# Two-layer hybrid encoder trunk: the split weight buffers begin at eight different 16-byte phases modulo 128 instead of one

## Chip, cores and metric

The kernel runs on one core of one Trainium2 chip. The metric is device time in microseconds of one execution, the median over the runs shown. Ahead of the launch the host only lays the inputs out in memory.

## The reference, cut to what matters

The input x is 512 tokens by 1024 channels in float32. Two layers follow each other, each a mixer and a gated MLP, all with residual adds, and a last RMSNorm. The outer structure, in which `even_mixer` and `odd_mixer` are attention layers with one combined input projection and one output projection each:

```python
h = x + even_mixer(rms_norm(x), w_in, w_out)     # layer 0: sparse top-k attention + chunked attention
h = h + conv_gated_ffn(rms_norm(h), w_up, conv_w, conv_b, w_down)
h = h + odd_mixer(rms_norm(h), w_in, w_out)      # layer 1: forgetting attention + windowed attention
h = h + conv_gated_ffn(rms_norm(h), ...)
y = rms_norm(h)

def conv_gated_ffn(x, w_up, conv_w, conv_b, w_down):
    h = x @ w_up                                  # 1024 -> 2 * 2816
    h = depthwise_causal_conv3(h, conv_w) + conv_b
    g, u = split(h, 2)
    return (silu(g) * u) @ w_down                 # 2816 -> 1024
```

What counts here is the dense products with weights: the input projections of the mixers, their output projections, and the up- and down-projections of the MLPs.

## The kernel before

Tokens lie along the free axis and channels on the partitions. Each product of two float32 matrices is made from three matmuls: both operands are split into a high part, rounded to the type that TensorE streams in one pass (float32r), and a low part, the remainder; `mm3` (L174 to L177) issues high x high at L175, then at L176 and L177 the two mixed products, into one PSUM bank.

**The weights.** `Stream` (from L114) walks a fixed plan of 196 weight tiles, each 128 partitions by up to 1024 words. `issue` loads one tile from HBM into `raw` (L132, two buffers, issued on SyncE), ScalarE copies it, rounded, into `whi` (L135), and VectorE subtracts that from `raw` into `wlo` (L137; for the keys `A1` and `kB`, eight tiles, GpSimd does it). There are four buffers for `whi` and four for `wlo`, used in turn. `ahead` keeps two tiles ready, `get` hands one out as a view of the columns in use. 188 tiles are 1024 words wide; four have 648 (two halves of 324, the indexer's projection, `"i"`) and four have 528 (two halves of 264, the narrow projection of layer 1, `"d"`).

**Who reads them.** In `tok_group` and `tok_wide` the activations `xT` are the stationary operand of the matmul and the weights stream by as the moving one, in rows of 512, 324 or 264 words. In `chan_mm`, `out_half` and the down-projection the weights are the stationary operand, in blocks of 128 x 128, and the activations (`xT`, `yT`, `VS`, `act`) stream by with 512 columns (256 in a few places). Each matmul instruction brings its own load of the stationary operand.

**The order of the work.** Every engine gets its instructions in the order in which the program writes them. In the mixers, dense matmuls are woven between the attention steps as fill (`weave`, `Fill`); in an MLP (`ffn`, from L702) one weight tile serves one block of 128 channels and 24 matmuls; `W.ahead(2)` stands ahead of each. The convolution of the MLP reads and writes with offsets of one and two words: `dst[:, 1:]` at L714 and `dst[:, 2:]` at L716.

**The memory.** Pools lie one behind the other in each partition. The pool of the weights holds `raw`, `whi` and `wlo`, every buffer 4096 bytes, and each of the eight split buffers begins at a multiple of 128 bytes.

Of the kernel before, what the change touches and what calls it, by code (L numbers as in the profile page):

```python
# [11 lines left out]
F32R = mybir.dt.float32r  # L12
# [73 lines left out]
def trunk(ctx, tc, a, out):  # L86
# [5 lines left out]
    wp = ctx.enter_context(tc.tile_pool(name="wts", bufs=4))  # L92
# [24 lines left out]
    class Stream:  # L117
# [4 lines left out]
        def issue(self):  # L122
            key = PLAN[self.pos]
            self.pos += 1
            if key[0] == "i":
                src, w = a["w_i"][key[1]], 2 * NI
            elif key[0] == "d":
                src, w = a["w_d"][key[1]], 2 * ND
            else:
                src, w = a["w"][WIDE_AT[key]], 1024  # L130
            raw = wp.tile([128, 1024], F32, name="raw", tag="raw", bufs=2)
            nc.sync.dma_start(raw[:, :w], src)  # L132
            hi = wp.tile([128, 1024], F32R, name="whi", tag="whi")
            lo = wp.tile([128, 1024], F32R, name="wlo", tag="wlo")
            nc.scalar.activation(hi[:, :w], raw[:, :w], AF.Copy)  # L135
            eng = nc.gpsimd if key[0] in ('A1', 'kB') else nc.vector
            eng.tensor_tensor(lo[:, :w], raw[:, :w], hi[:, :w].bitcast(F32), OP.subtract)  # L137
            self.ready[key] = (hi, lo)
# [1014 lines left out]
```

## Time and profile before

| what | us |
|---|---|
| runs shown | 1284.32 and 1286.52 |
| their median | 1285.42 |
| the profiled execution, its own time | 1287.78 |
| its span, first to last instruction | 1286.1 |

The mean granted clock of TensorE over that span is 0.986 of 2.4 GHz. All instruction times of the trace are from this one execution. PE is TensorE's matmuls, PEld its loads of the stationary operand, DVE is VectorE, ACT is ScalarE, POOL is GpSimd. Names are given as out<-in, and of a matmul's two inputs the moving one comes first. A matmul's record is longer than the spacing of the starts, because matmuls are pipelined; the spacing of the starts is the pace.

### The profile page before, as it was taken

The numbers are of one execution on the slowest core, as the hardware profiler recorded it, in microseconds if no ns is written. First come the engines' busy times: TensorE is split into PE (matmuls) and PEld (weight loads), VectorE is DVE, ScalarE is ACT, GpSimd is POOL, SyncE is SP. The second block draws the span as 40 slices with busy tenths as digits, with TensorE's granted clock in tenths as the row PEclk, the third lists the DMA queues.
The fourth block names the chain that finished last, engine by engine and source line by source line (L and its number), as shares of the span: only waits on it lengthen the run. The fifth ranks groups of instructions, "written<-read, shape, count | busy, mean of one in ns | idle before, by whom it ended". The sixth has DMA issues, their size and how long they took to land. (4 is left out here: it accounts for less than half of the span.)

```text
span 1286.1 us, 15902 instructions
## 1 busy us (share of the span) xinstructions
PE 1265.4 (98%) x5904; PEld 1024.6 (80%) x5904; DVE 826.1 (64%) x1524; ACT 594.0 (46%) x1008; POOL 198.5 (15%) x275
## 2 busy tenths in 40 slices
PE   8999999999999999999999999999999999999997
PEld 7767777777888888888888777778788888888886
DVE  7989865777777777743325566767777777772222
ACT  6545454555544444432224666666644444442221
POOL 3346331212000000000011334311200000000000
PEclk9989999999999999999999999889999999999999
DMA  6322122313223333332222311201333333322321
GB/s 208 85 79 83 34 66 66 99 34 98 86 98 98 99 98 99 96 91 96 96 67 81 115 49 34 66 17 51 100 98 99 99 98 99 96 93 92 98 81 66
DMA packets 34221, 109.61 MB, mean 85 GB/s; under 512 B 4064, under 2 KB 6496, under 8 KB 34144
## 3 DMA queue, kind: packets, MB, share of 16 engines
q1 hardware_dynamic: 34144, 108.60, 27.0%
q8 instruction: 46, 0.75, 0.2%
q14 instruction: 31, 0.25, 0.1%
HBM read 106.49 MB, written 2.10 MB: 84 GB/s over the span
## 5 line engine op out<-in xcount | busy, mean ns | idle before, releaser
L137 DVE TENSOR_TENSOR wlo<-raw,whi 128x1024 fp32r<-128x1024 f32 (+2 forms) x188 | 232.6, 1237 | 152.5 <-ACT whi L135 149.3
L135 ACT ACTIVATE whi<-raw 128x1024 fp32r<-128x1024 f32 (+2 forms) x196 | 204.8, 1045 | 224.3 <-PE acc L176 152.1
L175 PE MATMUL acc<-xT,whi 128*128 128x512 f32 x480 | 191.3, 399 | 0.4 <-ACT xT L229 0.4
L176 PE MATMUL acc<-xT,whi 128*128 128x512 f32 x480 | 188.3, 392 | 1.8 <-DVE xT L230 1.8
L177 PE MATMUL acc<-xT,wlo 128*128 128x512 f32 x480 | 188.0, 392 | 0.0
L212 POOL TENSOR_TENSOR scr<-scr,os 128x512 f32<-128x512 f32 x24 | 34.3, 1430 | 723.2 <-ACT os L210 723.2
L175 PE MATMUL acc<-act,whi 128*128 128x512 f32 (+1 forms) x374 | 140.9, 377 | 0.0
L177 PE MATMUL acc<-act,wlo 128*128 128x512 f32 (+1 forms) x374 | 140.9, 377 | 0.0
L176 PE MATMUL acc<-act,whi 128*128 128x512 f32 (+1 forms) x374 | 140.9, 377 | 0.0
L175 PE MATMUL s<-xT,whi 128*128 128x512 f32 x352 | 137.9, 392 | 0.0
L177 PE MATMUL s<-xT,wlo 128*128 128x512 f32 x352 | 137.0, 389 | 0.0
L176 PE MATMUL s<-xT,whi 128*128 128x512 f32 x352 | 137.0, 389 | 0.0
L175 PEld LDWEIGHTS acc<-xT,whi 128*128 128x128 f32 x480 | 90.8, 189 | 23.5 <-issue 4.8
L176 PEld LDWEIGHTS acc<-xT,whi 128*128 128x128 f32 x480 | 90.8, 189 | 19.9 <-DVE xT L230 2.5
L177 PEld LDWEIGHTS acc<-xT,wlo 128*128 128x128 f32 x480 | 90.6, 189 | 19.4
L175 PE MATMUL acc<-whi,xT 128*128 128x512 f32 (+2 forms) x208 | 84.5, 408 | 0.9 <-ACT whi L135 0.9
L177 PE MATMUL acc<-whi,xT 128*128 128x512 f32 (+2 forms) x208 | 80.7, 389 | 1.3 <-DVE xT L230 1.3
L712 DVE TENSOR_TENSOR ov<-s,R 128x512 f32<-128x512 f32 x44 | 30.4, 692 | 79.9 <-PE s L177 79.9
L182 ACT ACTIVATE act<-scr 128x512 fp32r<-128x512 f32 x44 | 27.8, 631 | 115.7 <-DVE scr L736 115.7
L176 PE MATMUL acc<-wlo,xT 128*128 128x512 f32 (+2 forms) x208 | 80.4, 387 | 0.6 <-DVE wlo L137 0.4
L176 PEld LDWEIGHTS acc<-act,whi 128*128 128x128 f32 x374 | 70.4, 188 | 13.0
L177 PEld LDWEIGHTS acc<-act,wlo 128*128 128x128 f32 x374 | 70.4, 188 | 13.0
(230 smaller groups left out, 2362.1 us busy)
## 6 DMA issues: line engine op xcount, KB each, us to landing
raw<-in_w SPq DMA_DIRECT2D x188, 512.0 KB, 3.5
h<-in_x SPq DMA_DIRECT2D x8, 256.0 KB, 4.1
T<-in_relb SPq DMA_DIRECT2D x8, 256.0 KB, 2.7
raw<-in_w_i SPq DMA_DIRECT2D x4, 324.0 KB, 3.4
raw<-in_w_d SPq DMA_DIRECT2D x4, 264.0 KB, 2.7
out_y<-h SPq DMA_DIRECT2D x4, 256.0 KB, 2.2
out_y<-h SPq DMA_DIRECT2D x2, 384.0 KB, 2.4
ropeC<-in_ropeC SPq DMA_DIRECT2D x2, 256.0 KB, 4.3
```

Of the source, the lines that this page charges most:

```text
L135: nc.scalar.activation(hi[:, :w], raw[:, :w], AF.Copy)
L137: eng.tensor_tensor(lo[:, :w], raw[:, :w], hi[:, :w].bitcast(F32), OP.subtract)
L175: nc.tensor.matmul(o, lh, rh, start=start, stop=False)
L176: nc.tensor.matmul(o, lh, rl, start=False, stop=False)
L177: nc.tensor.matmul(o, ll, rh, start=False, stop=stop)
L182: nc.scalar.activation(dh, src, AF.Copy)
L212: eng.tensor_tensor(ss, ss, sq, OP.add)
L712: nc.vector.tensor_tensor(v, o, R, OP.mult)
```

## The change

The two allocations of a split weight tile become 1040 words wide instead of 1024, and the tile in use is a view of 1024 words that begins 0, 4, 8 or 12 words (0, 16, 32 or 48 bytes) into the buffer. The offset goes to the next value after every fourth tile of the plan. All reads and writes of `whi` and `wlo` go through the view. The instructions, their order, their shapes and their waits are those of before.

```diff
             raw = wp.tile([128, 1024], F32, name="raw", tag="raw", bufs=2)
             nc.sync.dma_start(raw[:, :w], src)
-            hi = wp.tile([128, 1024], F32R, name="whi", tag="whi")
-            lo = wp.tile([128, 1024], F32R, name="wlo", tag="wlo")
+            o = 4 * (self.pos // 4 % 4)
+            hi = wp.tile([128, 1040], F32R, name="whi", tag="whi")[:, o:o + 1024]
+            lo = wp.tile([128, 1040], F32R, name="wlo", tag="wlo")[:, o:o + 1024]
             nc.scalar.activation(hi[:, :w], raw[:, :w], AF.Copy)
             eng = nc.gpsimd if key[0] in ('A1', 'kB') else nc.vector
             eng.tensor_tensor(lo[:, :w], raw[:, :w], hi[:, :w].bitcast(F32), OP.subtract)
```

## Rows read from the trace of the kernel before

**Rows 1.** The page: busy us of each engine, share of the span, instructions.

```profile
PE 1265.4 (98%) x5904; PEld 1024.6 (80%) x5904; DVE 826.1 (64%) x1524; ACT 594.0 (46%) x1008; POOL 198.5 (15%) x275
```

**Rows 2.** Windows in the first MLP's and second MLP's up-projection.

```profile
core 0: us, PE busy (x) PEld busy (x) DVE busy (x) ACT busy (x) POOL busy (x), PEclk, DMA share, GB/s
400.00:500.00 100.00, 100.00 (x443) 82.81 (x442) 73.15 (x92) 46.01 (x56) 0.00 (x0) 1.00 0.31 95
1000.00:1100.00 100.00, 100.00 (x443) 82.84 (x442) 72.62 (x92) 45.67 (x56) 0.00 (x0) 1.00 0.31 97
```

**Rows 3.** Timeline in the first down-projection, TensorE: start us, us, instruction.

```profile
600.05 0.39 PE L175 MATMUL acc<-act,whi 128*128 128x512 f32 x1
...
605.50 0.39 PE L175 MATMUL acc<-act,whi 128*128 128x512 f32 x1
```

**Rows 4.** Timeline in the last column block, with 256 columns, TensorE.

```profile
1273.72 0.28 PE L175 MATMUL acc<-act,whi 128*128 128x256 f32 x1
...
1275.16 0.28 PE L175 MATMUL acc<-act,whi 128*128 128x256 f32 x1
```

**Rows 5.** Instructions on the tile whi: count, ns minimum/median/maximum, first and last start.

```profile
L175 PEld LDWEIGHTS acc<-act,whi x374: 187/188/192, 552.2 to 1276.1; 128*128 128x128 f32 x187
L175 PEld LDWEIGHTS acc<-whi,xT x208: 186/188/192, 6.3 to 818.7; 128*128 128x128 f32 x104
```

**Rows 6.** Waits of TensorE: us in total, times, longest us.

```profile
PE s L175 <- ACT qk L493: 2.0, 1, 2.0
PE acc L176 <- DVE xT L230: 1.8, 2, 1.0
PE s L176 <- POOL qk L494: 1.6, 2, 1.0
...
PE acc L175 <- ACT whi L135: 0.9, 1, 0.9
...
PE acc L176 <- DVE wlo L137: 0.4, 1, 0.4
```

**Rows 7.** Timeline of both narrow projections, TensorE: halves begin at the acc rows.

```profile
20.05 0.31 PE L175 MATMUL acc<-whi,xT 128*128 128x324 f32 x1
...
21.70 0.31 PE L177 MATMUL s<-whi,xT 128*128 128x324 f32 x1
21.84 0.31 PE L175 MATMUL acc<-whi,xT 128*128 128x324 f32 x1
...
23.47 0.31 PE L177 MATMUL s<-whi,xT 128*128 128x324 f32 x1
...
675.04 0.28 PE L175 MATMUL acc<-whi,xT 128*128 128x264 f32 x1
...
676.48 0.28 PE L175 MATMUL acc<-whi,xT 128*128 128x264 f32 x1
...
677.93 0.28 PE L175 MATMUL acc<-whi,xT 128*128 128x264 f32 x1
```

**Rows 8.** Timeline of a stretch of 128-column matmuls, TensorE.

```profile
821.04 0.27 PE L176 MATMUL s<-kdT,qk 64*128 64x128 f32 x1
...
821.82 0.27 PE L177 MATMUL s<-kdT,qk 64*128 64x128 f32 x1
```

**Rows 9.** Groups by line and form: count, busy us, mean ns, idle before and releaser.

```profile
L137 DVE TENSOR_TENSOR wlo<-raw,whi 128x1024 fp32r<-128x1024 f32 x180 | 224.8, 1249 | 139.4 <-ACT whi L135 136.2
L716 DVE SCALAR_TENSOR_TENSOR scr<-ov,cw,scr 128x510 f32<-128x510 f32 x88 | 66.0, 750 | 3.0
L714 DVE SCALAR_TENSOR_TENSOR scr<-ov,cw,scr 128x511 f32<-128x511 f32 x88 | 65.6, 745 | 0.0
...
L187 DVE SCALAR_TENSOR_TENSOR VS<-acc,rs,VS 128x512 fp32r<-128x512 f32 x12 | 8.9, 747 | 10.2 <-ACT VS L186 10.2
...
L135 ACT ACTIVATE whi<-raw 128x1024 fp32r<-128x1024 f32 x188 | 199.3, 1060 | 207.7 <-PE acc L176 136.2 <-PE s L176 40.7 <-DMA raw<-in_w 9.4
```

**Rows 10.** Windows around the two falls of the granted clock; columns as in rows 2.

```profile
73.40:83.60 10.20, 9.18 (x23) 6.64 (x24) 6.47 (x23) 3.00 (x7) 2.66 (x4) 0.51 0.16 50
...
824.00:827.70 3.70, 3.32 (x19) 2.30 (x18) 3.27 (x12) 3.20 (x15) 0.94 (x2) 1.00 0.36 121
827.70:848.20 20.50, 20.50 (x55) 13.98 (x55) 9.62 (x39) 8.24 (x29) 4.23 (x8) 0.51 0.10 31
```

**Rows 11.** Timeline ahead of the first fall, TensorE; in brackets idle before and releaser.

```profile
70.96 0.39 PE L177 MATMUL acc<-xT,wlo 128*128 128x512 f32 x1
73.35 0.32 PE L175 MATMUL s<-qk 64*128 64x128 f32 x1 [2.00 <-ACT qk L493]
```

## The prediction

> **What bounds the kernel now.** I read the page's busy times first: TensorE is busy 1265.4 of 1286.1 us, no other compute engine over 826.1 [rows 1]. A busy matmul row is not yet a full one, so I went to the windows by stage. In the gated MLPs TensorE never stops: 443 records in 100 us, VectorE at 73, ScalarE at 46 [rows 2]. Then the timeline of the down-projection: from the start at 600.05 to the one at 605.50 lie 24 matmuls of 512 columns, so 5.45 / 24 = 227.1 ns apart [rows 3]. 512 columns at 2.4 GHz, the level granted there, are 213.3 ns, so about 13.7 ns per matmul are not streaming. With 256 columns twelve starts take 1.44 us, 120.0 ns, against 106.7 of streaming: again 13.3 ns [rows 4]. So there is a fixed part of 13 to 14 ns that doesn't grow with the columns; I read it as what is left exposed of putting in the next stationary block, since every matmul has its own load. The loads themselves take 188 ns at the median, 186 to 192, and run beside the matmul before [rows 5]. Other engines are waited for almost nowhere: the largest entries of TensorE's waits are 2.0, 1.8 and 1.6 us, and for a weight tile 0.9 and 0.4 us [rows 6]. The time is therefore (number of matmuls) x (columns + a fixed 13 to 14 ns), and a change moves it only if it changes that pace, or makes a weight tile come later than TensorE wants it.
>
> **The change part by part.** No instruction, wait or queue entry is added, removed or moved: the program issues the same instructions in the same order with the same semaphores. Only addresses differ. By the code, a buffer was 4096 bytes, 32 x 128, so all eight began at the same place modulo 128. Now it is 1040 x 4 = 4160 bytes, 32 x 128 + 64, so neighbours alternate between phases 0 and 64; the offset adds 0, 16, 32 or 48 bytes, one value for four tiles. Of the 196 tiles 24 to 26 fall on each of the eight phases, so 7 in 8 move. Eight buffers grow by 64 bytes: what is allocated behind them lies 512 bytes higher, a multiple of 128, so no other operand changes its phase. The loads from HBM go into raw, which doesn't move. Four kinds of access see the new phases.
>
> (a) A weight tile as moving operand: from the code, 6 token-major projections x 4 token tiles x 8 x 3 = 576 matmuls of 512 columns, and 2 x 32 x 3 = 192 narrow ones. Here the trace already holds a shifted case. In the first projection the tile has two halves of 324 words, the second beginning at 1296 bytes, 16 modulo 128; in the second layer's narrow one at 1056 bytes, 32 modulo 128. The rows give both: at 264 columns the unshifted half takes 676.48 - 675.04 = 1.44 us for twelve, 120.0 ns, and the shifted half 677.93 - 676.48 = 1.45 us, 120.8 ns; at 324 columns eleven starts take 1.65 us unshifted and 1.63 us shifted, 150.0 and 148.2 ns [rows 7]. So a shift costs between -1.8 and +0.8 ns, which is the rounding of the rows. 576 x 7/8 x these is -0.9 to +0.4 us. I take 0.
>
> (b) A weight tile as stationary operand: up 2 x 44 x 24 = 2112, down 2 x 528 plus 66 for a column split in halves = 1122, output halves 420, channel-major projections 16 x 24 = 384, together 4038. No load from a shifted address is in the trace, so this is bounded from both sides. The nearest rows are those of (a), shifted reads by the same engine: 0. How much a slower load could hide comes from a stretch of 128-column matmuls: from 821.04 to 821.82 seven starts, 111 ns apart, though 128 columns stream in 53 ns [rows 8]. There the load sets the pace, about one per 111 ns. Under a 512-column matmul the load may thus grow from 111 to 227 ns, to 2.04 times, before it shows; a shift that added one part in eight to each load stays out of sight. If it were uncovered, its price is the fixed part: between vanishing and doubling, 4038 x 7/8 x 13.4 ns = 47 us either way. I take 0, because the nearest row says 0 and because of this slack, and keep both ends as rivals.
>
> (c) The split of raw: ScalarE writes the high part (1060 ns for 1024 words), VectorE reads it and writes the low part (1249 ns) [rows 9]; eight tiles go to GpSimd. For VectorE shifted rows exist: the convolution's updates start 4 and 8 bytes into their tiles and take 745 and 750 ns for 511 and 510 words; the unshifted update of the same kind with 512 words takes 747 ns [rows 9]. So 0. For ScalarE's write there is no shifted row. Its bounds are nothing and, generously, the whole length again. Even that is covered in the MLP: 19 tiles per 100 us x 1.06 = 20 us on top of ScalarE's 46.0 [rows 2]; the same on VectorE gives 73.2 + 19 x 1.25 = 97 of 100. A tile would be ready 1 to 2.5 us later, and two are kept ahead at 24 matmuls, 5.4 us, each. Where that cover is missing, at the first tiles, TensorE waited 0.9 and 0.4 us [rows 6]; some 5 us in all is my upper estimate from four narrow tiles at about 1 us. I take 0.
>
> The sum is 0 + 0 + 0. The profiled execution took 1287.8 us with a span of 1286.1 us, and keeps both; it lies 2.4 us above the median of the two timed runs, 1285.4 us. The forecast for the median is 1285.4 us. About 2% (25.7 us) is what a measurement of this kernel can tell from no change.
>
> **The rivals.** *Slower: the exposed part grows.* If a stationary block that doesn't begin at a multiple of 128 is fetched in more pieces, the load is no longer hidden. Its place is the 3533 shifted loads (7/8 of 4038); it decides from a pace of 226.7 + 25.7 us / 3533 = 234 ns, that is, a load 2.1 times as long as the 111 ns of rows 8. A doubled fixed part gives 1285.4 + 47 = 1333 us. For it: TensorE has no idle time in the MLPs to absorb anything, and no row shows such a load. Against it: the slack, and (a), where the same engine reads shifted rows at the old pace. The Trainium skill, TensorE: Matmul & The Clock Gate, LDWEIGHTS (loading the stationary operand), says a load goes by its columns alone, about 107 ns at 128 by its formula, and names no alignment; the 111 ns of rows 8 agree with the length, no run here shows the rest yet, and by that page this rival gives 0.
>
> *Faster: the fixed part is a collision that goes away.* All the weights and all moving operands begin at 0 modulo 128 now; if load and stream met in the same place of the memory and the 13 to 14 ns were that stall, spreading the phases could save up to the same 47 us, 1238 us. For it: the constant is there in every matmul. Against it: it is the same for 512 and 256 columns [rows 3, 4], where a collision would grow with the time that both read, and shifting the moving side alone took nothing off [rows 7]. The Trainium skill, SBUF — State Buffer, Who interferes with whom, gives TensorE two independent read ports, one for the stream and one for loads, so that nothing would be there to relieve; that agrees with rows 7, and by it this rival gives 0.
>
> *The clock's two falls move.* The granted clock was 0.51, the 1.2 GHz level, for 10.2 us from 73.4 and for 20.5 us from 827.7 [rows 10]. Before the first, TensorE had waited 2.0 us at 71 to 73 us [rows 11]; before the second it was busy 3.32 of 3.70 us with short matmuls [rows 10]. Half of each stretch is lost: 5 and 10 us. If a few tens of ns of drift dropped both, the time would be 1270 us, if it added as many, 1301 us; both are within 2%. Against it: with unchanged durations the waits before both falls are unchanged, and the three executions lie within 3.5 us.
>
> *The phases are not what the text says*, say because an allocator rounds each buffer up to 128 bytes: then four phases remain instead of eight, every price above stays at its taken value, and the time is again 1285.4 us.
>
> **How the numbers follow.** No change by (a) to (c), the allocator's rounding with it: 0.87, its own range 1279 to 1294 us (the runs' spread of 3.5 us, (c)'s 5 us, (a)'s 1 us). Falls of the clock moved: 0.06, 1270 to 1301 us. Slower by the load: 0.04. Faster by the collision: 0.03. A range from 1278 to 1297 us leaves out less than 2 in 10 and takes in (c)'s bound and part of the clock's. Faster by over 2%: 0.03; within 2%: 0.93; slower by over 2%: 0.04.
>
> **What would show it.** Right: in the changed kernel's profile TensorE's starts in the MLPs stay 227 ns apart, about 443 records per 100 us; loads stay at 186 to 192 ns; the two splits stay near 1060 and 1249 ns; all tiles of a stage show one pace, whatever their phase. (b) is wrong if the spacing differs between groups of eight matmuls that read different buffers, or if the loads' median leaves 188 ns. (c) is wrong if the split on ScalarE or VectorE gets longer, and it matters only if TensorE's waits for whi or wlo grow past a few us. The prediction as a whole fails if the pace in the MLPs moves by more than 4.5 ns.

## The result and the profile after

The changed kernel took 1301.68 us (1300.79 and 1302.57) against 1285.42 us: 1.0127 times the time of before, with an interval of 1.0079 to 1.0174. It is slower, by more than the measurement is uncertain and by less than 2%. The profiled execution took 1302.57 us with a span of 1300.9 us.

The page of the changed kernel shows where the time does not lie. VectorE, ScalarE and GpSimd are as busy as before, and the number of instructions is the same; TensorE's busy time alone rose, from 1265.4 to 1282.0 us [rows 1].

```profile
PE 1282.0 (99%) x5904; PEld 1025.4 (79%) x5904; DVE 827.3 (64%) x1524; ACT 590.9 (45%) x1008; POOL 198.7 (15%) x275
```

The windows in the two up-projections answer to [rows 2]; the columns are those named there. TensorE is busy all the time, as before, at the full clock, as before, but it starts 434 matmuls in 100 us where it started 443.

```profile
400.00:500.00 100.00, 100.00 (x434) 81.19 (x434) 71.84 (x91) 43.79 (x55) 0.00 (x0) 1.00 0.30 95
1000.00:1100.00 100.00, 100.00 (x434) 81.30 (x433) 71.79 (x91) 43.87 (x56) 0.00 (x0) 1.00 0.31 95
```

The timeline of TensorE in the first down-projection answers to [rows 3]. The rows shown are the first matmuls of six weight tiles that follow each other; 24 matmuls lie from each to the next. (In the changed kernel all lines stand one further down, L176 for L175; in the runs below the three lines of `mm3` can stand lower still.)

```profile
555.28 0.39 PE L176 MATMUL acc<-act,whi 128*128 128x512 f32 x1
...
560.73 0.39 PE L176 MATMUL acc<-act,whi 128*128 128x512 f32 x1
...
566.23 0.40 PE L176 MATMUL acc<-act,whi 128*128 128x512 f32 x1
...
571.82 0.39 PE L176 MATMUL acc<-act,whi 128*128 128x512 f32 x1
...
577.38 0.39 PE L176 MATMUL acc<-act,whi 128*128 128x512 f32 x1
...
582.83 0.40 PE L176 MATMUL acc<-act,whi 128*128 128x512 f32 x1
```

The five tiles take 5.45, 5.50, 5.59, 5.56 and 5.45 us, that is 227.1, 229.2, 232.9, 231.7 and 227.1 ns per matmul. The allocator hands the four buffers out in the order 0, 3, 2, 1 (so the addresses in the built program), and with the offset added the five tiles begin 0, 192, 128, 80 and 16 bytes into a stretch of 256 bytes. So the first and the last run at the old pace and the three between don't: the pace belongs to the tile.

The loads on `whi`, TensorE's waits for weights and the two splits answer to [rows 5], [rows 6] and [rows 9]. First the instructions on the tile whi (count, ns minimum/median/maximum, first and last start), the loads after and the matmuls that they serve, before and after:

```profile
L176 PEld LDWEIGHTS acc<-act,whi x374: 187/188/193, 555.0 to 1290.9; 128*128 128x128 f32 x187
```

```profile
L175 PE MATMUL acc<-act,whi x374: 278/389/389, 552.5 to 1276.2; 128*128 128x512 f32 x165, 128*128 128x256 f32 x22
```

```profile
L176 PE MATMUL acc<-act,whi x374: 278/392/404, 555.3 to 1291.0; 128*128 128x512 f32 x165, 128*128 128x256 f32 x22
```

Then TensorE's waits after, of which these two are for weight tiles, and the groups by line and form:

```profile
PE acc L176 <- ACT whi L136: 1.6, 1, 1.6
...
PE acc L177 <- DVE wlo L138: 0.4, 1, 0.4
```

```profile
L138 DVE TENSOR_TENSOR wlo<-raw,whi 128x1024 fp32r<-128x1024 f32 x180 | 224.8, 1249 | 145.5 <-ACT whi L136 143.2
...
L136 ACT ACTIVATE whi<-raw 128x1024 fp32r<-128x1024 f32 x188 | 199.3, 1060 | 222.5 <-PE acc L177 145.9 <-PE s L177 45.9 <-DMA raw<-in_w 12.6
```

A load's record is 188 ns as before, the splits take 1060 and 1249 ns as before, and no wait for a weight tile is longer than 1.6 us. Only the matmuls' records grew, from 389 to 392 ns at the median. Nothing comes late; TensorE itself is slower while it works.

To see for which matmuls, I worked out the pace from the starts in the trace: the time from one start to the next, for the 512-column matmuls that have a weight block as stationary operand and `xT` or `act` as the stream (up- and down-projections and channel-major projections, some 3390 starts without those followed by a pause). Its mean is 226.9 ns before and 231.6 ns after. Sorted by the place of the stationary block modulo 256 bytes (four buffers at a pitch of 4160 bytes, times four offsets, are sixteen places), the changed kernel gives the following; every place rests on some 190 to 235 matmuls. The streams `xT` and `act` all begin at 0 modulo 256, as they did before.

| place of the block, bytes modulo 256 | mean pace, ns |
|---|---|
| 240, 0, 16 | 227.1, 227.3, 227.4 |
| 32, 48, 64, 80 | 233.2, 233.1, 233.2, 232.0 |
| 96, 112, 128, 144, 160 | 234.1, 233.3, 232.7, 233.5, 233.4 |
| 176, 192 | 230.1, 229.3 |
| 208, 224 | 232.1, 233.5 |

The sums over the starts of both traces account for the loss: with `act` streaming 990 x (231.17 - 226.67) = 4.5 us, with `xT` 2454 x (235.43 - 230.91) = 11.1 us (here with the pauses), with weights streaming 518 x (243.27 - 240.87) = 1.2 us, with `yT` and `VS` 0.5 us, in the narrow and 256-column matmuls -1.2 us; together 16.1 us. Each span times its mean granted clock, which takes out what the falls of the clock cost, gives 1300.9 x 0.988 - 1286.1 x 0.986 = 17.2 us.

### The profile page after: what moved, and what is told of

It reads as the page before. It is cut to its first block, busy times and chain, and to the rows that moved or that the text cites. A ratio compares the mean times of both kernels' runs of the same rounds, so it can differ in the third digit from the quotient of the medians.

```text
span 1300.9 us, 15902 instructions
## 1 busy us (share of the span) xinstructions
PE 1282.0 (99%) x5904; PEld 1025.4 (79%) x5904; DVE 827.3 (64%) x1524; ACT 590.9 (45%) x1008; POOL 198.7 (15%) x275
## 5 line engine op out<-in xcount | busy, mean ns | idle before, releaser
L138 DVE TENSOR_TENSOR wlo<-raw,whi 128x1024 fp32r<-128x1024 f32 (+2 forms) x188 | 234.9, 1249 | 159.4 <-ACT whi L136 157.1
L176 PE MATMUL acc<-xT,whi 128*128 128x512 f32 x480 | 193.4, 403 | 0.1
L177 PE MATMUL acc<-xT,whi 128*128 128x512 f32 x480 | 190.6, 397 | 1.5 <-DVE xT L231 1.5
L176 PE MATMUL acc<-act,whi 128*128 128x512 f32 (+1 forms) x374 | 142.2, 380 | 0.0
L176 PE MATMUL s<-xT,whi 128*128 128x512 f32 x352 | 139.6, 397 | 0.0
L177 PE MATMUL s<-xT,whi 128*128 128x512 f32 x352 | 138.7, 394 | 0.0
L176 PEld LDWEIGHTS acc<-xT,whi 128*128 128x128 f32 x480 | 91.0, 189 | 24.8 <-issue 4.5
L176 PE MATMUL acc<-whi,xT 128*128 128x512 f32 (+2 forms) x208 | 85.1, 411 | 1.6 <-ACT whi L136 1.6
L176 PEld LDWEIGHTS acc<-act,whi 128*128 128x128 f32 x374 | 70.3, 188 | 14.4
L177 PEld LDWEIGHTS acc<-act,whi 128*128 128x128 f32 x374 | 70.3, 188 | 14.2
```

Of the source, the lines that this page charges most:

```text
L176: nc.tensor.matmul(o, lh, rh, start=start, stop=False)
L177: nc.tensor.matmul(o, lh, rl, start=False, stop=False)
```

## The experiments

Four theories stood against each other at first. A: the place of the stationary block relative to the streaming operand, modulo 256, sets the pace. B: the absolute place of the stationary block does. C: any operand away from a multiple of 256 costs. D: the change of place from tile to tile costs. Most runs are one execution beside one of the kernel before on the same chip. Since the falls of the clock differ from execution to execution, I compare the pace, worked out as above, and the span of the profiled execution times its mean granted clock ("at full clock"; where there are several runs of before, against their median); the clock has three digits, so the latter is good to about 1 us.

| run | time, us (before on the same chip) | pace, ns | at full clock, more than before on that chip, us |
|---|---|---|---|
| e1_weights_at_64 | 1296.05 (1278.81) | 233.3 | 22.3 |
| e2_activations_at_64 | 1289.29 (1278.81) | 229.0 | 9.2 |
| e3_both_at_64 | 1282.93 (1278.81) | 226.9 | 1.5 |
| e4_phase_map | 1299.74 (1278.81) | 232.2 | 19.5 |
| e5_low_parts_at_64 | 1294.82 (1279.94) | 231.1 | 12.2 |
| e6_wlo_at_64 | 1296.71 (1279.94) | 231.1 | 11.5 |
| e7_low_streams_at_64 | 1298.72 (1279.94) | 232.0 | 13.5 |
| e8_pitch_alone | 1293.47 (1279.94) | 230.7 | 10.8 |
| e9_alternate_with_k | 1302.65 (1281.67) | 232.2 | 17.4 |
| e10_change_again | 1302.15 (1281.67) | 231.6 | 16.0 |
| e11_both_at_64_timed | 1282.42 (1281.67) | 226.9 | -1.4 |
| e12_weights_at_128 | 1305.57 (1281.77) | 232.4 | 15.8 |

The 22.3 us of the first row are 3390 x (233.3 - 226.9) = 21.7 us of pace, and the other rows agree with theirs in the same way to within 4 us.

### All weights at one other place, all activations, both

The first edit puts 64 bytes of unused memory ahead of the four `whi` and 192 behind the eight buffers, so that every weight block lies at 64 modulo 256 and everything behind them where it was:

```diff
             nc.sync.dma_start(raw[:, :w], src)
+            if self.pos == 1:
+                wp.tile([128, 16], F32, name="pad0", tag="pad0", bufs=1)
             hi = wp.tile([128, 1024], F32R, name="whi", tag="whi")
             lo = wp.tile([128, 1024], F32R, name="wlo", tag="wlo")
+            if self.pos == 1:
+                wp.tile([128, 48], F32, name="pad1", tag="pad1", bufs=1)
```

> Against the kernel before: all eight weight buffers begin at 64 modulo 256 and stay there; nothing else changes its phase. In the changed kernel the MLP tiles at 64 modulo 256 ran at 233.1 ns per matmul against 226.7 at 0. Theory A (relative: what counts is where the stationary block begins modulo 256 against where the streaming operand begins, which is 0 here) expects 233 ns in every MLP tile, some 3100 x 6.4 = 20 us, so 1302 to 1311 us. Theory B (absolute: the stationary block's own place modulo 256) expects the same. Theory C (any of the two operands off a multiple of 256 costs) expects the same. Theory D (what costs is that the phase changes from tile to tile) expects a steady 226.7 ns and 1283 to 1289 us.

The second leaves the weights alone and moves the activations, `xT` and `act`, by 64 bytes:

```diff
-    xT = [xp.tile([128, KD, SEQ], F32R, name=f"xT{i}") for i in range(2)]
+    xT = [xp.tile([128, KD * SEQ + 64], F32R, name=f"xT{i}")[:, 16:16 + KD * SEQ]
+          .rearrange("p (a b) -> p a b", a=KD) for i in range(2)]
...
+            fp.tile([128, 16], F32, name="pad2")
             act = [fp.tile([128, 2, SEQ], F32R, name=f"act{j}") for j in range(NFF)]
+            fp.tile([128, 48], F32, name="pad3")
```

> Against the kernel before: the weights stay at 0 modulo 256, but the operands that stream by in the MLPs (xT and act) begin at 64 modulo 256. Theory A (relative) expects the pace of a difference of -64, that is 192 modulo 256, where the changed kernel had 229.2 ns: about 3100 x 2.5 = 8 us, so 1290 to 1297 us. Theory B (the stationary block's own place) expects 226.7 ns and 1283 to 1289 us. Theory C (any operand off) expects about what the weights at 64 cost, 1302 to 1311 us. Theory D expects 1283 to 1289 us.

The third makes both edits.

> Against the kernel before: the weights and the streaming operands xT and act all begin at 64 modulo 256. Theory A (relative) expects 226.7 ns again in the MLPs and 1283 to 1290 us, although no operand there lies at a multiple of 256. Theories B and C expect 233 ns or more and 1302 to 1311 us. Theory D expects 1283 to 1289 us.

Windows over the first MLP and over the second, TensorE alone (us, busy with the count of matmuls, granted clock, DMA share, GB/s). First the kernel before:

```profile
340.00:640.00 300.00, 300.00 (x1326) 1.00 0.31 97
960.00:1240.00 280.00, 280.00 (x1237) 1.00 0.31 98
```

The weights alone at 64:

```profile
340.00:640.00 300.00, 300.00 (x1287) 1.00 0.30 94
960.00:1240.00 280.00, 280.00 (x1201) 1.00 0.30 94
```

The activations alone at 64:

```profile
340.00:640.00 300.00, 300.00 (x1313) 1.00 0.30 97
960.00:1240.00 280.00, 280.00 (x1225) 1.00 0.31 96
```

Both at 64:

```profile
340.00:640.00 300.00, 300.00 (x1326) 1.00 0.30 98
960.00:1240.00 280.00, 280.00 (x1237) 1.00 0.31 98
```

Moved alone, either operand costs matmuls, 39 of 1326 or 13; moved together, not one is lost. B falls (the same weights at the same place are slow in the first run and fast in the third), C falls (third run), D falls (in the first run all tiles have one place and the pace is the slow one). A holds in size too: with the activations 64 bytes further the block lies at 192 modulo 256 relative to the stream, and 229.0 ns was measured where the table of the changed kernel has 229.3 for a block at 192. The three times, however, lie below the ranges of theory A, 1296.05 against 1302 to 1311, 1289.29 against 1290 to 1297 and 1282.93 against 1283 to 1290 us: the ranges start from some 1285 us for the kernel before, which took 1278.81 us beside these runs.

### The pitch without the offset

One part of the change alone. Theory A1 in the expectation is a narrower form of A: the block against the stream that runs while it is loaded (more of it below).

```diff
-            o = 4 * (self.pos // 4 % 4)
-            hi = wp.tile([128, 1040], F32R, name="whi", tag="whi")[:, o:o + 1024]
-            lo = wp.tile([128, 1040], F32R, name="wlo", tag="wlo")[:, o:o + 1024]
+            hi = wp.tile([128, 1040], F32R, name="whi", tag="whi")
+            lo = wp.tile([128, 1040], F32R, name="wlo", tag="wlo")
```

> One part of the change alone: buffers of 1040 words, no offset inside, so the four buffers of each kind begin at 0, 64, 128 and 192 modulo 256. Theory A1 expects the changed kernel's paces of these four places tile by tile, 227.1, 233.1, 232.7 and 229.2 ns, mean 230.5 ns in the MLPs, and about 1289 to 1297 us on this chip. A theory in which the 16-byte offsets are what costs expects 226.7 to 227 ns.

Measured 230.7 ns: the places 0, 64, 128 and 192 have 227.4, 233.3, 232.8 and 229.3 ns. The pitch of 4160 bytes by itself brings (230.7 - 226.9) / (231.6 - 226.9), about eight tenths of the loss; the offset adds the rest: it brings half of the tiles of the one good buffer to slow places (32 and 48) and half of those of the buffer at 192 to slower ones (208 and 224), more than those at 80, 176 and 240 gain.

### Half of the period

All weights at 128 modulo 256, the first edit with 32 and 32 words in place of 16 and 48.

> Against the kernel before: all eight weight buffers begin at 128 modulo 256, so they still begin at a multiple of 128 bytes, as all buffers of the kernel before do. Theory A with a period of 256 expects the changed kernel's pace of that place, 232.7 ns in the MLPs, and 1293 to 1304 us against 1278 to 1285. If the period were 128, 226.7 to 227.0 ns and 1278 to 1286 us.

```profile
340.00:640.00 300.00, 300.00 (x1293) 1.00 0.30 95
960.00:1240.00 280.00, 280.00 (x1206) 1.00 0.31 96
```

Again fewer matmuls in these windows, 1293 and 1206, and a pace of 232.4 ns. A multiple of 128 bytes is not enough; the period is not 128. The time, 1305.57 us, lies a little above the expected range; the granted clock was 0.986 in this run and 0.992 in the one beside it. Nor is the period longer than 256: in the run with the pitch alone the four `whi` take 4 x 4160 = 16640 bytes, 256 more than a multiple of 512, so a tile's `wlo` lies 256 bytes off its `whi` modulo 512, and at place 0 the blocks of both have the good pace, 227.5 and 227.3 ns.

### A finer map

The offset steps through sixteen words of 4 bytes instead of four steps of 16 bytes; with the four buffers that makes 64 places.

```diff
-            o = 4 * (self.pos // 4 % 4)
+            o = (self.pos - 1) // 4 % 16
```

> Against the changed kernel: the same buffers, but the offset goes through all sixteen words of a 64-byte piece, so the tiles take every one of the 64 word places modulo 256, each at least once in both MLPs. Theories A, B and C expect the pace of a tile to be a function of its place modulo 256, the same in both MLPs and equal to the changed kernel's at the sixteen places it had: 226.8 to 227.1 ns at 240, 0 and 16, 229 to 234 elsewhere, and a time near 1301 us (1297 to 1305). Theory D expects no such function and every tile slow. If any place is faster than 226.7 ns, a version that beats both kernels exists; I expect none.

Each place has 30 to 72 matmuls. Fast, 226.8 to 227.4 ns, are 0, 16, 120, 132, 156 and 252; 240 has 228.8; the others lie between 229.1 and 237.6, most of them at 233. The map is jagged (164 has 237.6 ns, 156 has 226.9), so no simple distance explains it; the places that it shares with the changed kernel repeat that one's values to 0.8 ns but for 240, which has 1.7 ns more. The expectation named too few fast places, and its 229 to 234 ns elsewhere was too narrow at the top. No place is faster than the old one, so with 512 columns there was nothing to be won from the weights' place.

### Which of the two meetings counts

While a matmul streams, the next block is loaded, and later a stream flows through that block (in the kernel before, the matmul of L175 starts at 600.05 us and the load for the one of L176 at 600.06). A1: what counts is the place of the block against the stream that runs while it is loaded. A2: its place against the stream that later flows through it. Three runs and a fourth mix the places so that A1 and A2 differ. The first of them puts `wlo` and the low parts of `xT` and `act` at 64 and leaves the high parts at 0; then, in the order of `mm3`, every load runs beside a stream at its own place. The other two make half of that edit each:

```diff
             hi = wp.tile([128, 1024], F32R, name="whi", tag="whi")
+            if self.pos == 1:
+                wp.tile([128, 16], F32, name="pad0", tag="pad0", bufs=1)
             lo = wp.tile([128, 1024], F32R, name="wlo", tag="wlo")
...
-    xT = [xp.tile([128, KD, SEQ], F32R, name=f"xT{i}") for i in range(2)]
+    xT = [xp.tile([128, KD, SEQ], F32R, name="xT0"),
+          xp.tile([128, KD * SEQ + 64], F32R, name="xT1")[:, 16:16 + KD * SEQ]
+          .rearrange("p (a b) -> p a b", a=KD)]
...
-            act = [fp.tile([128, 2, SEQ], F32R, name=f"act{j}") for j in range(NFF)]
+            ahi = [fp.tile([128, SEQ], F32R, name=f"acth{j}") for j in range(NFF)]
+            fp.tile([128, 16], F32, name="pad2")
+            alo = [fp.tile([128, SEQ], F32R, name=f"actl{j}") for j in range(NFF)]
...
```

> Against the kernel before, in the MLPs: wlo begins at 64 modulo 256, and so do the low parts of the streaming operands (xT1, the low halves of act); whi and the high parts stay at 0. The order is: whi with the high part, whi with the low part, wlo with the high part; and each block's load starts with the matmul ahead of it. Theory A1 (what counts is the block being loaded against the operand streaming at that moment) then has a difference of 0 for every load (whi under the high part, wlo under the low part, whi under the high part) and expects 226.7 to 227.3 ns in the MLPs and 1276 to 1285 us on this chip. Theory A2 (a block against the operand that later streams through it) has differences of 0, -64 and +64 in turn and expects 228 to 232 ns, 1283 to 1296 us.

> Control for the run with the low parts at 64: wlo alone begins at 64 modulo 256, all else stays at 0. Theories A1 and A2 both have one load in three at a difference of 64 and expect more than 228 ns in the MLPs, at most 233.3; by a third of 6.4 ns 228.8 ns, about 1283 to 1298 us.

> The second control: the low parts of the streaming operands alone begin at 64 modulo 256, all weights and the high parts stay at 0. A1 has the load of wlo at a difference of -64, A2 the second whi; both expect 227.3 to 229.0 ns in the MLPs, about 1279 to 1290 us.

The first has 231.1 ns: A1 alone falls, since by it nothing should have changed. The second has 231.1 ns, over the 228.8 of a plain third but under the upper end of 233.3; the third has 232.0 ns and 1298.72 us, outside what was expected (at most 229.0 ns and 1290 us). By the lines of `mm3`, the second has 228.4, 229.3 and 235.6 ns. The timeline of it, TensorE in the down-projection, shows the long one on `wlo` itself: 0.23, 0.23 and 0.24 us after the three starts of a group.

```profile
605.01 0.39 PE L179 MATMUL acc<-act,whi 128*128 128x512 f32 x1
605.24 0.39 PE L180 MATMUL acc<-act,whi 128*128 128x512 f32 x1
605.47 0.40 PE L181 MATMUL acc<-act,wlo 128*128 128x512 f32 x1
605.71 0.39 PE L179 MATMUL acc<-act,whi 128*128 128x512 f32 x1
```

But the other two, whose own block and stream were not moved, are slower than 226.9 as well; beside one of them, that of L180, runs the load of `wlo`, beside the other nothing that was moved. The fourth run gives every matmul a stream and a block at one place, and changes the place with every channel block: even k at 0, odd k at 64 (the buffers of the attention's `PT` go from three to two to make room).

```diff
-            hi = wp.tile([128, 1024], F32R, name="whi", tag="whi")
-            lo = wp.tile([128, 1024], F32R, name="wlo", tag="wlo")
+            hi = wp.tile([128, 1088], F32R, name="whi", tag="whi")
+            lo = wp.tile([128, 1088], F32R, name="wlo", tag="wlo")
...
+                return [Blocks([x[:, 528 * (i % 2) + 128 * (i // 2):528 * (i % 2) + 128 * (i // 2) + 128]
+                                for i in range(8)]) for x in (hi, lo)]
...
+        xT.append(Blocks([t_[:, 2064 * (c % 2) + 512 * (c // 2):2064 * (c % 2) + 512 * (c // 2) + 512]
+                          for c in range(KD)]))
```

> Against the kernel before, in the MLPs: the 128-channel blocks alternate. For even k the weight blocks and the streaming operands (high and low) begin at 0 modulo 256, for odd k all of them at 64; so a block always lies at the same place as the operand that streams through it, but where k changes (one matmul in three) its load runs beside a stream that lies 64 away. (Two buffers instead of three for the transposed probabilities make room; that touches the attention alone, so the pace in the MLPs is what is read, not the time.) The run with the low parts at 64 has already spoken against theory A1 as the whole story: every load matched the stream beside it, and the pace was 231.1 ns. Theory A2 (a block against the operand that streams through it) expects 226.7 to 227.3 ns in the MLPs. Theory A4 (a block must match both the stream beside its load and the stream through it; 226.7 needs one place for all neighbours) expects 228.5 to 233 ns, as in the runs where one load in three was off.

Measured 232.2 ns, so A2 alone falls too. What is left is that the fast pace was seen where all operands that follow each other kept one relation, as in the kernel before and in the third run. How exactly the reads of one matmul reach into the pace of the next was not tried further and stays open.

### The change and the third run again, timed

> The changed kernel itself, beside the run with weights and streams at 64, for an interval on one chip. Theory A (relative place modulo 256) expects what the first measurement gave, 1.010 to 1.017 times the kernel before.

> Weights, xT and act all at 64 modulo 256, timed. Theory A (relative) expects 0.998 to 1.004 times the kernel before; a theory in which the weights' own place counts expects 1.015 to 1.022.

Timed again beside the kernel before, the change gives 1302.15 us (1301.16 to 1302.55), 1.0158 times before [1.0137, 1.018], and the same sixteen paces to within 0.7 ns. The third run's kernel gives 1282.42 us, 1.0003 times before [0.9988, 1.0018]: moving weights and activations together takes back the whole loss.

## Why the prediction was wrong

**The bound and the sum's form were right.** Time is the number of matmuls times their pace, and the waits did not change. The text named what would refute it, a pace in the MLPs moved by more than 4.5 ns; in the MLPs alone it went from 226.7 to 231.6 ns, by 4.9.

**Term (b) failed.** It was taken as 0, with bounds of 47 us either way, and measured 15.6 us (4.5 + 11.1) on the blocks against `xT` and `act`, 16.1 with `yT` and `VS`. The step that failed is the choice of the nearest row: "the nearest rows are those of (a), shifted reads by the same engine: 0". Those rows are narrow matmuls, and narrow matmuls answer otherwise. In them the weights stream and `xT` is the block, so a half shifted by 16 or 32 bytes puts the block at 240 or 224 modulo 256. With 512 columns 240 is a fast place in any case (227.1 ns), and 224 costs 6.6 ns (233.5 - 226.9); the 264-column row showed 0.8 ns for it. In the run with the activations at 64 the block `xT` lies 64 ahead of the weights. There the 512-column matmuls of the token-major projections go from 229.4 to 233.2 ns, the 324-column ones stay at 148 ns, and of the 264-column ones, answering to [rows 7], the first half of a tile takes 122.5 ns and the second 120.8 (120.0 and 120.8 before):

```profile
680.14 0.28 PE L175 MATMUL acc<-whi,xT 128*128 128x264 f32 x1
...
681.61 0.29 PE L175 MATMUL acc<-whi,xT 128*128 128x264 f32 x1
...
683.06 0.28 PE L175 MATMUL acc<-whi,xT 128*128 128x264 f32 x1
```

With 256 columns the sign is even reversed. In the run with the weights at 64, in the last column block, answering to [rows 4]:

```profile
1271.44 0.28 PE L179 MATMUL acc<-act,whi 128*128 128x256 f32 x1
...
1272.80 0.28 PE L179 MATMUL acc<-act,whi 128*128 128x256 f32 x1
```

Twelve matmuls take 1.36 us, 113.3 ns each, where they took 120.0. (In the second half of the columns, at the same places modulo 256, they take 117.8 ns; what sets the two paces apart was not tried.) So the row was almost blind to what was asked of it: in the changed kernel both halves of the 264-column tiles still take 121.2 ns.

**The fixed part was misread.** I read the 13 to 14 ns as one constant because 512 and 256 columns had the same [rows 3, 4]. Moved by 64 bytes the two part: 20.0 ns over the streaming time with 512 columns (233.3 - 213.3), 6.6 ns with 256 (113.3 - 106.7), or 11.1 in the second half of the columns. The equality held at the one place that the kernel before used, and was no sign that this part is independent of what both operands read.

**The slack did not protect.** The stretch of [rows 8] said that a load may get twice as long before it shows. The load's record stayed at 188 ns and the pace got worse all the same; what grew is the matmul's record (389 to 392 ns at the median), not the load's. The rival "slower by the load" had the right side, place and part of the price (16 of its 47 us), but the mechanism that it named, a load that outgrows its cover, is not what the trace shows. Nor is it shifted against 128: of its eight phases seven were said to move, but of the sixteen places that matter three kept the pace, and 128 modulo 256 was among the slow ones.

**The rival "collision" had the picture upside down.** It took the common place for the collision and the spread for the cure. With 512 columns the common place is the best one found, and spreading the places brought the loss. I weighed a rule of the Trainium skill there, SBUF — State Buffer, Who interferes with whom, by which TensorE's two read ports are independent. The runs disagree with what I drew from it, that the places don't matter: 226.9 and 233.3 ns differ only by the relation of the two operands' places. By what path the two meet isn't shown. The Trainium skill, TensorE: Matmul & The Clock Gate, LDWEIGHTS (loading the stationary operand), has a load go by its columns and names no alignment. The record of a load agrees in this, 188 ns at the median in every run; the pace of load and matmul together doesn't.

**The rest held.** (c): both splits kept their lengths, the first waits for weights are 1.6 and 0.4 us. (a): 1.2 us on 518 matmuls, above its bound of 0.4 us, because here, too, the price was taken from narrow rows. The falls of the clock cost 1300.9 x 0.012 = 15.6 us against 1286.1 x 0.014 = 18.0, and explain nothing of the loss. The allocator kept the pitch of 4160 bytes and the offsets, as the paces by place show, so the fourth rival did not come up.

## What to carry to other kernels

Keep the stationary blocks and the streams of long matmuls at one common place modulo 256 bytes (here 0 and 64 were tried, with the same pace), and look at the pitch of a pool as well as at its start: 64 bytes more per buffer cost this kernel about 11 us. When TensorE has no idle time, measure its pace tile by tile: a pace that changes exactly where the buffer changes points to a place in memory, though no load's record is longer and no wait appears. And take the price of an edit from a row of the same shape; the narrow matmuls of this kernel would have shown next to nothing.

## What was not expected of the hardware

- The pace of a 512-column matmul with its own load depends on the relation of the two operands' places modulo 256 bytes: 226.9 ns at the same place, 229.0 to 229.3 with the block 192 bytes ahead, 233.3 with 64; in steps of 4 bytes, from 226.8 to 237.6 ns.
- With 256 columns the order is reversed: 120.0 ns at the same place, 113.3 to 117.8 ns with the block 64 bytes ahead. There are 204 such matmuls here, so at most 204 x 6.7 ns = 1.4 us would be to win, less than these measurements can tell; no run was made for it.
- Mixed places cost more than the sum of their pairs: with only `wlo` moved the mean is 4.2 ns up, twice a third of 6.4, since also the two matmuls that don't use it slow down, to 228.4 and 229.3 ns. By what path is open.
